# A two-layer decoder trunk: the norm's root applied ahead of the FFN's up products, the embedding's input product moved in front of them, and the convolution fed from PSUM

## Chip, cores and metric

The kernel runs on one core of one Trainium2 chip, in one launch. The metric is the device time of that core in microseconds; lower is better. A run before took 1123.33 us (median of three, 1122.11 to 1124.11).

## The reference, cut to what matters

The trunk has two layers over 512 positions with 1024 features (22 x 128 = 2816 in the FFN), all in float32. Layer 0 mixes by a gated MLP with spatial gating, layer 1 by sliding-window attention. Each layer then runs the same two blocks, and these are what the change touches:

```python
def rmsnorm(x, g):
    y = x * lax.rsqrt(jnp.mean(x * x, axis=-1, keepdims=True) + EPS)
    return y * g

def conv_ffn(xn, w_up, conv_w, conv_b, w_down):          # xn = rmsnorm(h, norm_ffn)
    h = xn @ w_up                                        # 1024 -> 2 * 2816
    hp = jnp.pad(h, ((0, 0), (CONV_WIDTH - 1, 0), (0, 0)))
    c = conv_b + sum(hp[:, t:t + S] * conv_w[t] for t in range(CONV_WIDTH))
    g, u = jnp.split(c, 2, axis=-1)
    return (jax.nn.silu(g) * u) @ w_down

def per_layer_embed(h, p_i, g_norm, w_in, w_gate, b_gate):
    gate = jax.nn.sigmoid(rmsnorm(h, g_norm) @ w_gate + b_gate)
    return (p_i @ w_in) * gate                           # added to h
```

The product `p_i @ w_in` depends on no other step of the layer, so it can be computed anywhere ahead of the gate.

## The kernel before, in words

**Layout and products.** Activations lie transposed, 128 features on the partitions by 512 positions: `h[0..7]` is the residual stream. Each float32 operand is split into a high part rounded to the matmul's type and a low remainder, and a product is three matmuls (high x high, low activation x high weight, high activation x low weight), all in `mm3`. The weight splits come out of `pump`: ACT casts the high part (`wh`, L197), DVE subtracts for the low part (`wl`, L198), 1024 columns at a time. Four buffers hold such pairs (WBUFS), three the raw weights. `plan` lists the weight pieces in the order of their use, and `load` and `pump` walk down that list, some units ahead of the products, on the SP queue. The order of instructions on each engine is made by a scheduler from the order in which the code issues them; `behind` adds an order by hand.

**The norm.** `Norm.take(k)` runs as each `h[k]` is finished: it splits `h[k]` times the gain into the tiles `xs` (ACT L302, DVE L303), squares it on ACT and adds up the squares (POOL, the last one on DVE). `turn` transposes and reduces the sum (`nf0quarter`), and `begin` sums over the partitions by a small matmul (`nf0ms`) and takes the root on POOL (`nf0rt`). The root belongs to a position, thus to a column of every tile, and must reach all partitions. `spread` does that with a matmul by ones into PSUM (`np0sp`); with `line=True` the root goes to HBM and comes back to all partitions by two DMAs of POOL (`nf0line`, `nf0rstd`). The FFNs used the second way: up products ran on input without the root, and each result was multiplied by the root afterwards.

**The FFN** (`ffn`) has 22 up products of 48 matmuls (24 for the gate half, 24 for the other half, each into its own PSUM bank). `gated` turns two banks into one activation: DVE multiplies by the root (`hs`, L551), ACT starts the convolution with the last tap and the bias (`c`, L557), DVE adds the two other taps (L558, L559), ACT applies silu, DVE multiplies the halves (`a`, L563). The down products come in three parts: after up 0 to 7 and up 8 to 15 in a woven form that saves multiplications (`woven_add`, products `dx` and `dy` of 256 columns), after up 16 to 21 as plain products (`dense_add`, `d`). One up product is always issued ahead of a woven part, to cover the last gate.

**The embedding.** `ple_in` (layer 0, products `pin`) and `ple_in_rows` (layer 1, `pint`) compute `p @ w_in` in 48 matmuls between up 21 and the `d` products, and ACT copies the results to `m0` to `m3` in SBUF, where they stay until the gate stage (`ple`, or the final stage of layer 1) multiplies them. The tiles `m0` to `m3` also hold operands of the woven products, and `m4`, `m5` the split input `p`.

Of the kernel before, what the change touches and what calls it, by code (L numbers as in the profile page):

```python
# [13 lines left out]
P = 128  # L14
# [36 lines left out]
def tile_yoco(ctx: ExitStack, tc: tile.TileContext, t, out: bass.AP, out_b: bass.AP):  # L51
# [29 lines left out]
    def plan_cols(w, n_chunks, kk, cols=256, k0=0):  # L81
        for c in range(n_chunks):
            plan(w[c, :, k0 * cols : (k0 + kk) * cols], kk * cols, cols)
# [11 lines left out]
            pieces.append((w[c, :, k0 * 256 : k1 * 256], 2 * n, [(0, n)] * 3 + [(0, n // 2)], None))  # L95

    def plan_ffn(l):
        for i, (j0, j1) in enumerate(PARTS):
            if i == 0:
                plan_cols(t["w_up"][l], j1, KD)  # L100
            else:
                plan_cols(t["w_up"][l, j0 + 1 : j1], j1 - j0 - 1, KD)
            if i + 1 < len(PARTS):
                plan_cols(t["w_up"][l, j1 : j1 + 1], 1, KD)
            else:
                plan(t["pT"][l], 2 * S, S, own=[(mp, "m4", "m5")])
# [211 lines left out]
    class Norm:  # L318


        def __init__(self, name, gains):
            self.name = name
# [64 lines left out]
        def spread(self, c0, n):  # L387

            d = tp.tile([P, n, 64], F32R, tag="acc", name=f"{self.name}d")
            nc.vector.tensor_mul(d, pick.rearrange("p (o t) -> p o t", o=1).to_broadcast([P, n, 64]),  # L390
                                 self.hl[:, c0 : c0 + n].bitcast(F32).rearrange("p (c o) -> p c o", o=1)
                                 .to_broadcast([P, n, 64]))
# [138 lines left out]
    def ffn(l, norm, nxt):  # L531

        xs = norm.xs[0][0]
        rstds = []
# [12 lines left out]
        def gated(j, pss, fronts=()):  # L547
            cs = []
            for s, ps in enumerate(pss):
                hs = tp.tile([P, S], F32, tag="hs", name=f"hs{j}_{s}")  # L550
                ins = nc.vector.tensor_mul(hs, ps, rstds[1])  # L551
                if fronts:
                    behind(ins, splits[fronts[s]][1])
# [3 lines left out]
                nc.scalar.activation(c, hs, AF.Identity, bias=v("conv_b", l * 2 * NJ + col), scale=cw[2])  # L557
                nc.vector.scalar_tensor_tensor(c[:, 1:], hs[:, : S - 1], cw[1], c[:, 1:], op0=ALU.mult, op1=ALU.add)  # L558
# [4 lines left out]
            nc.vector.tensor_mul(a, a, cs[1])  # L563
# [27 lines left out]
        return pe  # L591

    def ple_in(l):
        pw = chunk(S, 2)
        px = [(a[:, o : o + S], b[:, o : o + S]) for a, b, o in pw]
        pe = []
        for c in range(2):
            parts = chunk(256, 4)
            for q in range(2):
                pq = mp.tile([P, 2, S], F32, tag=f"m{2 * c + q}", name=f"pe{c}_{q}")  # L600
                for j in range(2):
                    ps = psum(f"pin{c}_{q}_{j}")
                    mm3(ps, parts[2 * q : 2 * q + 2], px, j * P)
                    nc.scalar.copy(pq[:, j, :], ps)
                    pe.append(pq[:, j, :])
        return pe

    def ple_in_rows():

        pw = chunk(S, 2)  # L610
        px = [(a[:, o : o + S], b[:, o : o + S]) for a, b, o in pw]
# [1 line left out]
        for c in range(2):  # L613
# [3 lines left out]
            for i in range(NC):  # L617
# [7 lines left out]
        return tok  # L625

    def ple(l, norm, nxt, pe):
        xs = norm.xs[0][0]
# [118 lines left out]
    for c in range(4):  # L747
# [4 lines left out]
        for j in range(2):  # L752
# [332 lines left out]
            with tc.high_priority():  # L1085
                weights(i)
    state["tags"] = [0, 1, 2]
    nf = Norm("nf1", [(xp, "x", gain("norm_ffn", 1))])
# [269 lines left out]
```

## Time and profile before

| what | us |
|---|---|
| median of three runs | 1123.33 |
| lowest, highest | 1122.11, 1124.11 |
| the profiled execution, its own time | 1120.52 |
| its span, first to last instruction | 1118.8 |

The profile is of one execution, and all times of rows are counted from its span's start. Some stages of it, in us from the start: the up products of layer 0 from 143.8, those of layer 1 from 700.3; pin at 465.45, pint at 1022.22. The granted clock of TensorE is 0.998 over the span. A row of a group gives engine, line, operation, output and inputs, then the number of instructions, their busy time, the mean in ns, and the idle time of the engine just before them with what ended it. A row of a timeline gives start, duration, engine, line, operation, tiles and shapes. A row of the chain of waits gives start, duration and what ran. A row of the stretches gives the stretch, its length, the busy time of PE, its weight loads, DVE, ACT and POOL with their counts, the clock, the DMA engines' share and GB/s. PE rows overlap: a matmul's duration goes to the end of its output, and the next begins before that.

### The profile page before, as it was taken

To read this page: it belongs to the slowest core of one execution; us is meant where nothing else is said; L and a number is where in the kernel's file an instruction comes from. 1 tells how busy PE (TensorE), PEld (TensorE's weight loads), DVE (VectorE), ACT (ScalarE), POOL (GpSimd) and SP (SyncE) were. 2 spreads that over 40 slices of the span, in tenths; PEclk is the share of its full clock that TensorE was granted. 3 is DMA by queue.
4 is the path that set the end of the run, shared out by engine and by line. 5 is a ranking of instruction groups with operands and counts; after the bars stand their busy time and mean duration, and the time that the engine had idled before them with its cause. 6 is when DMAs were issued, how large, how long until landed. Compare 5 with 4: busy or idle time off the path is not lost.

```text
span 1118.8 us, 14875 instructions
## 1 busy us (share of the span) xinstructions
PE 1108.8 (99%) x5691; PEld 947.1 (85%) x5691; DVE 868.3 (78%) x1374; ACT 568.9 (51%) x936; POOL 103.9 (9%) x167
## 2 busy tenths in 40 slices
PE   9999999999999999999999999999999999999997
PEld 7888888889888998888888887888898889988876
DVE  5566449999788877657988997499997898785696
ACT  5733325545444544554656776255454445445543
POOL 1100210000000000022204451100000000000210
PEclk9999999999999999999999999999999999999999
DMA  8632313223331252333134224321244212522433
GB/s 296 135 114 76 113 48 113 76 76 123 142 113 39 76 189 69 101 113 113 63 88 132 76 57 151 111 93 71 76 151 136 90 38 76 189 85 88 148 103 86
DMA packets 35624, 118.40 MB, mean 106 GB/s; under 512 B 11800, under 2 KB 17440, under 8 KB 25056
## 3 DMA queue, kind: packets, MB, share of 16 engines
q1 hardware_dynamic: 34800, 116.19, 31.8%
q0 software_dynamic: 336, 0.79, 0.4%
q8 instruction: 45, 0.74, 0.3%
q10 hardware_dynamic: 416, 0.46, 0.1%
q14 instruction: 27, 0.22, 0.1%
HBM read 109.02 MB, written 2.11 MB: 99 GB/s over the span
## 4 chain that ended last, share of the span: by engine, by line
PE 68%; DVE 20%; ACT 4%; DMA 4%; issue 3%; POOL 0%; POOLq 0%; SPq 0%; ACTq 0%; DVEq 0%
PE up L229 26%; PE d L229 7%; PE dx L229 5%; DVE wl L198 5%; PE dy L229 4%; PE gate L229 4%; PE u L229 4%; PE q L229 3%; DVE c L558 3%; DVE c L559 2%; PE o L229 2%; DVE hs L551 2%; ACT wh L197 1%; PE v L241 1%; PE v L239 1%
## 5 line engine op out<-in xcount | busy, mean ns | idle before, releaser
L198 DVE TENSOR_TENSOR wl<-wraw,wh 128x1024 fp32r<-128x1024 f32 (+2 forms) x198 | 232.8, 1177 | 83.4 <-ACT wh L197 82.1
L197 ACT CAST wh<-wraw 128x1024 fp32r<-128x1024 f32 (+2 forms) x197 | 194.1, 990 | 147.9 <-PE up L229 56.1
L229 PE MATMUL up<-nf00h,wh 128*128 128x512 f32 x352 | 137.1, 390 | 0.0
L229 PE MATMUL up<-nf10h,wh 128*128 128x512 f32 x352 | 137.0, 389 | 0.0
L229 PE MATMUL up<-nf10l,wh 128*128 128x512 f32 x352 | 137.0, 389 | 0.0
L229 PE MATMUL up<-nf00l,wh 128*128 128x512 f32 x352 | 137.0, 389 | 0.0
L229 PE MATMUL up<-nf00h,wl 128*128 128x512 f32 x352 | 136.9, 389 | 0.0
L229 PE MATMUL up<-nf10h,wl 128*128 128x512 f32 x352 | 136.9, 389 | 0.0
L557 ACT ACTIVATE c<-hs,vec 128x512 f32<-128x512 f32 x88 | 71.6, 815 | 64.4 <-DVE hs L551 62.6
L558 DVE SCALAR_TENSOR_TENSOR c<-hs,vec,c 128x511 f32<-128x511 f32 x88 | 65.5, 747 | 20.4 <-ACT c L557 20.4
L229 PEld LDWEIGHTS up<-nf10h,wh 128*128 128x128 f32 x352 | 66.1, 188 | 13.7
L229 PEld LDWEIGHTS up<-nf00h,wl 128*128 128x128 f32 x352 | 66.1, 188 | 13.7
L229 PEld LDWEIGHTS up<-nf10l,wh 128*128 128x128 f32 x352 | 66.1, 188 | 13.7
L229 PEld LDWEIGHTS up<-nf00l,wh 128*128 128x128 f32 x352 | 66.1, 188 | 13.6
L229 PEld LDWEIGHTS up<-nf00h,wh 128*128 128x128 f32 x352 | 66.1, 188 | 13.6
L229 PEld LDWEIGHTS up<-nf10h,wl 128*128 128x128 f32 x352 | 66.1, 188 | 13.5
L559 DVE SCALAR_TENSOR_TENSOR c<-hs,vec,c 128x510 f32<-128x510 f32 x88 | 65.6, 748 | 2.2
L197 ACT CAST wh<-wsum 128x1024 fp32r<-128x1024 f32 x32 | 33.7, 1052 | 35.3 <-PE dy L229 11.3
L551 DVE TENSOR_TENSOR hs<-up,nf1rstd 128x512 f32<-128x512 f32 x44 | 30.1, 686 | 21.1 <-DMA nf1rstd<-nf1line 10.5
L551 DVE TENSOR_TENSOR hs<-up,nf0rstd 128x512 f32<-128x512 f32 x44 | 30.1, 686 | 20.9 <-DMA nf0rstd<-nf0line 10.4
L198 DVE TENSOR_TENSOR wl<-wsum,wh 128x1024 fp32r<-128x1024 f32 x32 | 39.1, 1221 | 9.3 <-ACT wh L197 9.2
L562 ACT ACTIVATE a<-c 128x512 f32<-128x512 f32 x44 | 27.7, 630 | 15.9 <-DVE c L559 15.8
(519 smaller groups left out, 2661.4 us busy)
## 6 DMA issues: line engine op xcount, KB each, us to landing
wraw<-in_w_up SPq DMA_DIRECT2D x44, 1024.0 KB, 4.8
wraw<-in_w_down SPq DMA_DIRECT2D x16, 1024.0 KB, 4.8
wraw<-in_w_gate SPq DMA_DIRECT2D x8, 1024.0 KB, 5.3
wraw<-in_w_down SPq DMA_DIRECT2D x8, 768.0 KB, 4.1
wraw<-in_w_u SPq DMA_DIRECT2D x4, 1024.0 KB, 10.8
wraw<-in_w_out SPq DMA_DIRECT2D x4, 1024.0 KB, 4.7
wraw<-in_w_q SPq DMA_DIRECT2D x4, 1024.0 KB, 4.8
wraw<-in_w_o SPq DMA_DIRECT2D x4, 1024.0 KB, 4.9
```

The lines of the kernel that those rows point to most:

```text
L197: cast = nc.scalar.copy(hi, src)
L198: state["split"] = splits[u] = cast, nc.vector.tensor_sub(low, src, hi.bitcast(F32))
L229: nc.tensor.matmul(ps, w, x, start=first and j == 0, stop=last and j == len(todo) - 1, skip_group_check=onto)
L239: nc.tensor.matmul(ps, xh[:, s], wh[:, a:b], start=st, stop=False)
L241: nc.tensor.matmul(ps, xh[:, s], wl[:, a:b], start=False, stop=en)
L551: ins = nc.vector.tensor_mul(hs, ps, rstds[1])
L557: nc.scalar.activation(c, hs, AF.Identity, bias=v("conv_b", l * 2 * NJ + col), scale=cw[2])
L558: nc.vector.scalar_tensor_tensor(c[:, 1:], hs[:, : S - 1], cw[1], c[:, 1:], op0=ALU.mult, op1=ALU.add)
L559: nc.vector.scalar_tensor_tensor(c[:, 2:], hs[:, : S - 2], cw[0], c[:, 2:], op0=ALU.mult, op1=ALU.add)
L562: nc.scalar.activation(a, cs[0], AF.Silu)
```

## The change

1. The FFN's norms are made with `late=True` and no longer split `h` as it is finished. A new `Norm.scale` spreads the root by a matmul (`nf0sp`), and for each of the eight tiles DVE computes `x = h * gain * root` with the root read from PSUM, ACT copies the high part, DVE subtracts the low part. The two DMAs through `nf0line` are gone.
2. `pin` and `pint` are issued in front of up 0. `begin` stands after 18 of their 48 matmuls, `scale` after 36. The plan of weights moves accordingly.
3. Their results go from `m0` to `m3` to HBM (`keep`, DMAs on ACT's queue) and come back (`back`, DMAs on SP's queue, issued after up 18).
4. Up 0 runs through its eight inputs once and feeds both PSUM banks at each, where it ran all eight for one bank and then for the other. The order within an input is high activation with both weights, then the low activation.
5. `gated` has no `hs`: ACT and DVE read the up products from PSUM.
6. After up 21 the `d` products follow directly.

```diff
     def plan_ffn(l):
+        plan(t["pT"][l], 2 * S, S, own=[(mp, "m4", "m5")])
+        plan_cols(t["w_pin"][l], 2, 4)
...
-            else:
-                plan(t["pT"][l], 2 * S, S, own=[(mp, "m4", "m5")])
-                plan_cols(t["w_pin"][l], 2, 4)
...
         def take(self, k):
-            self.split(k, 0)
+            if not self.late:
+                self.split(k, 0)
...
+        def scale(self):
+            ps = self.spread(0, S // 64)
+            xs, g = self.xs[0]
+            u = state["next"]
+            for k in range(KD):
+                x = tp.tile([P, S], F32, tag="hs", name=f"{self.name}x{k}")
+                ins = nc.vector.scalar_tensor_tensor(x, h[k], g(k), ps, op0=ALU.mult, op1=ALU.mult)
+                if k % 4 == 0:
+                    behind(ins, splits[u + k // 4][1])
+                nc.scalar.copy(xs[k][0], x)
+                self.low = nc.vector.tensor_sub(xs[k][1], x, xs[k][0].bitcast(F32))
+            behind(splits[u + 2][1], self.low)
...
         def up(j, later=False):
             parts = chunk(256, KD)
-            pss = []
-            for s in range(2):
-                ps = psum(f"up{j}_{s}")
-                mm3(ps, parts, xs, s * P)
-                pss.append(ps)
-                if j == 0:
-                    rstds.append(norm.rstd() if s else norm.begin(rows=0, halves=False, line=True))
+            pss = [psum(f"up{j}_{s}") for s in range(2)]
+            if j:
+                for s in range(2):
+                    mm3(pss[s], parts, xs, s * P)
+            else:
+                for k, ((wh, wl, off), (xh, xl)) in enumerate(zip(parts, xs)):
+                    for x, both in ((xh, (wh, wl)), (xl, (wh,))):
+                        for s, ps in enumerate(pss):
+                            for w in both:
+                                nc.tensor.matmul(ps, w[:, off + s * P : off + (s + 1) * P], x,
+                                                 start=k == 0 and x is xh and w is wh, stop=k == KD - 1 and x is xl)
...
         def gated(j, pss, fronts=()):
...
-                hs = tp.tile([P, S], F32, tag="hs", name=f"hs{j}_{s}")
-                ins = nc.vector.tensor_mul(hs, ps, rstds[1])
...
-                nc.scalar.activation(c, hs, AF.Identity, bias=v("conv_b", l * 2 * NJ + col), scale=cw[2])
-                nc.vector.scalar_tensor_tensor(c[:, 1:], hs[:, : S - 1], cw[1], c[:, 1:], op0=ALU.mult, op1=ALU.add)
-                nc.vector.scalar_tensor_tensor(c[:, 2:], hs[:, : S - 2], cw[0], c[:, 2:], op0=ALU.mult, op1=ALU.add)
+                nc.scalar.activation(c, ps, AF.Identity, bias=v("conv_b", l * 2 * NJ + col), scale=cw[2])
+                for tap in (1, 2):
+                    ins = nc.vector.scalar_tensor_tensor(c[:, tap:], ps[:, : S - tap], cw[2 - tap], c[:, tap:],
+                                                         op0=ALU.mult, op1=ALU.add)
...
-        pe = None
+        kept = (ple_in_rows if l else ple_in)(l, norm)
         ahead = up(0)
+        behind(splits[state["next"] + 1][1], norm.low)
...
-            act += [whole(j - j0 - 1, j, up(j)) for j in range(j0 + 1, j1)]
-            pe = ple_in_rows() if l else ple_in(l)
+            for j in range(j0 + 1, j1):
+                act.append(whole(j - j0 - 1, j, up(j)))
+                if j == j0 + 2:
+                    back = [mp.tile([P, D], F32, tag=f"m{q}", name=f"back{q}") for q in range(NC)]
+                    for x, y in zip(back, kept):
+                        nc.sync.dma_start(x, y)
             dense_add(act, j1 - j0, nxt)
...
+    def keep(x, name):
+        y = dram.tile([P, D], F32, name=name)
+        nc.scalar.dma_start(y, x)
+        return y
...
     def ple_in(l, norm):
...
+                    if (c, q, j) == (0, 1, 0):
+                        norm.begin(rows=0)
+                    if (c, q, j) == (1, 0, 1):
+                        norm.scale()
+                pe.append(keep(pq, f"kept{c}_{q}"))
...
-    nf = Norm("nf0", [(xp, "x", gain("norm_ffn", 0))])
+    nf = Norm("nf0", [(xp, "x", gain("norm_ffn", 0))], late=True)
...
-            nf.split(m, 0)
             nf.square(m, nc.vector)
```

In the built program the order on the engines follows: after up 21, ACT casts two units of down weights ahead of the second `c`, and DVE makes their low parts ahead of its taps. In layer 0, ACT has the cast for up 2 ahead of the high parts of inputs 5, 6 and 7; in layer 1 it stands behind all eight. The loads of `back` stand on SP ahead of those for up 20 and 21.

More of the change, by code (lines that the diff above doesn't have):

```diff
@@ L318, in tile_yoco, with __init__ @@
     class Norm:
-        def __init__(self, name, gains):
-            self.name = name
+        def __init__(self, name, gains, late=False):
+            self.name, self.late = name, late
             self.xs = [(xtiles(pool, f"{name}{i}", tags), g) for i, (pool, tags, g) in enumerate(gains)]
@@ L556, in gated @@
                 c = tp.tile([P, S], F32, tag=f"c{s}", name=f"c{j}_{s}")
-                nc.scalar.activation(c, hs, AF.Identity, bias=v("conv_b", l * 2 * NJ + col), scale=cw[2])
-                nc.vector.scalar_tensor_tensor(c[:, 1:], hs[:, : S - 1], cw[1], c[:, 1:], op0=ALU.mult, op1=ALU.add)
-                nc.vector.scalar_tensor_tensor(c[:, 2:], hs[:, : S - 2], cw[0], c[:, 2:], op0=ALU.mult, op1=ALU.add)
+                nc.scalar.activation(c, ps, AF.Identity, bias=v("conv_b", l * 2 * NJ + col), scale=cw[2])
+                for tap in (1, 2):
+                    ins = nc.vector.scalar_tensor_tensor(c[:, tap:], ps[:, : S - tap], cw[2 - tap], c[:, tap:],
+                                                         op0=ALU.mult, op1=ALU.add)
+                    if fronts and tap == 1:
+                        behind(ins, splits[fronts[s]][1])
                 cs.append(c)
@@ L587, in ffn, with ple_in @@
             act = [whole(SLOTS - 1, j0, ahead)]
-            act += [whole(j - j0 - 1, j, up(j)) for j in range(j0 + 1, j1)]
-            pe = ple_in_rows() if l else ple_in(l)
-            dense_add(act, j1 - j0, nxt)
-        return pe
-    def ple_in(l):
+            for j in range(j0 + 1, j1):
[4 more added lines that the diff above has]
+                        nc.sync.dma_start(x, y)
+            dense_add(act, j1 - j0, nxt)
+        return back if l else [x[:, o : o + S] for x in back for o in (0, S)]
+    def keep(x, name):
+        y = dram.tile([P, D], F32, name=name)
+        nc.scalar.dma_start(y, x)
+        return y
+    def ple_in(l, norm):
         pw = chunk(S, 2)
@@ L599, in ple_in @@
             for q in range(2):
[L600 removed]
+                pq = mp.tile([P, D], F32, tag=f"m{2 * c + q}", name=f"pe{c}_{q}")
                 for j in range(2):
@@ L603, in ple_in, with ple_in_rows @@
                     mm3(ps, parts[2 * q : 2 * q + 2], px, j * P)
-                    nc.scalar.copy(pq[:, j, :], ps)
-                    pe.append(pq[:, j, :])
+                    nc.scalar.copy(pq[:, j * S : (j + 1) * S], ps)
+                    if (c, q, j) == (0, 1, 0):
[3 more added lines that the diff above has]
+                pe.append(keep(pq, f"kept{c}_{q}"))
         return pe
-    def ple_in_rows():
+    def ple_in_rows(l, norm):
         pw = chunk(S, 2)
@@ L624, in ple_in_rows @@
                 nc.scalar.copy(tok[i][:, c * S : (c + 1) * S], ps)
-        return tok
+                if (c, i) == (0, 2):
+                    norm.begin(rows=0)
+                if (c, i) == (1, 1):
+                    norm.scale()
+        return [keep(x, f"kept{i}") for i, x in enumerate(tok)]
     def ple(l, norm, nxt, pe):
@@ L1087, in tile_yoco @@
     state["tags"] = [0, 1, 2]
-    nf = Norm("nf1", [(xp, "x", gain("norm_ffn", 1))])
+    nf = Norm("nf1", [(xp, "x", gain("norm_ffn", 1))], late=True)
     for c in range(4):
```

3 lines of the change are left out of this document (removed).

## The prediction

> **What bounds the kernel now.** I read the page's head first, then the waits of TensorE (PE), then the chain that ended last, then the timelines of the places that the diff touches.
>
> ```profile
> span 1118.8 us, 14875 instructions
> PE 1108.8 (99%) x5691; PEld 947.1 (85%) x5691; DVE 868.3 (78%) x1374; ACT 568.9 (51%) x936; POOL 103.9 (9%) x167
> PE np1ms L361 <- DVE np1quarter L352: 0.5, 1, 0.5
> PE dy L229 <- DVE h L513: 0.4, 1, 0.4
> 283.25 87.07 PE up L229 x384
> 465.61 11.12 PE pin L229 x48
> ```
>
> PE is busy for 99% of the span, and the two longest waits that the profile names inside the work are 0.5 and 0.4 us. So the end is set by the number of matmuls and by the few places where PE stands still; no other engine's load counts by itself. The chain gives the rate: eight up products are 384 matmuls in 87.07 us, 0.227 us each (a single row shows 0.39 us because neighbours overlap). An up product of 48 takes 10.88 us, the embedding's input product (pin) 11.12 us. In the FFNs I compare the start of each matmul with the one before. Ahead of a dy or dx product six gaps are longer than the rate explains. The largest and the last are:
>
> ```profile
> 804.06 0.28 PE L229 MATMUL dx<-act,wl 128*128 128x256 f32 x1
> 804.79 0.39 PE L229 MATMUL dy<-act_0h,wh 128*128 128x256 f32 x1 [0.45 <-DVE h L513]
> 944.75 0.28 PE L229 MATMUL dy<-act_0l,wh 128*128 128x256 f32 x1
> 945.11 0.39 PE L229 MATMUL dx<-act_2h,wh 128*128 128x256 f32 x1
> ```
>
> A 256-column matmul follows the one before by 0.12 us, so these are 0.61 and 0.24 us lost; the other four lose 0.22 or 0.23 each. All six make 1.8 us, and that is all that a lighter VectorE (DVE) can give back to PE in both FFNs.
>
> **What goes, and why it is worth little.** Removed are the 88 products hs (all on DVE) and, per FFN, two DMAs of POOL that carried the root to all partitions; added per FFN are eight products x and one spreading matmul.
>
> ```profile
> L551 DVE TENSOR_TENSOR hs<-up,nf0rstd 128x512 f32<-128x512 f32 x44 | 30.1, 686 | 20.9 <-DMA nf0rstd<-nf0line 10.4 <-PE up L229 10.3
> L557 ACT ACTIVATE c<-hs,vec 128x512 f32<-128x512 f32 x88 | 71.6, 815 | 64.4 <-DVE hs L551 62.6
> L829 DVE SCALAR_TENSOR_TENSOR qf<-q,qscale,n1rstd 128x512 f32<-128x512 f32 x8 | 6.0, 748 | 1.2 <-PE q L229 1.1
> L558 DVE SCALAR_TENSOR_TENSOR c<-hs,vec,c 128x511 f32<-128x511 f32 x88 | 65.5, 747 | 20.4 <-ACT c L557 20.4
> L604 ACT COPY pe<-pin 128x512 f32<-128x512 f32 x8 | 4.7, 582 | 2.7 <-PE pin L229 2.7
> ```
>
> That is 60.2 us off DVE (44 x 0.686, twice), some 12 us back (16 x 0.75), and none of it was on PE. Even DVE's 10.4 us wait for the root cost PE nothing: no gap lies there. Of the 1.8 us above I credit half, **-0.9** (bounds 0 and -1.8), since such a gap can also be a weight that is only just prepared. The taps now read PSUM. A scalar_tensor_tensor of this size takes 748 ns where its source is the PSUM product (qf) and 747 where it is SBUF (c), so I price that at zero. [...]
>
> The two spreading matmuls are pure PE work: 2 x 0.227 = **+0.45**. The 96 matmuls of pin only move. The four new DMAs to HBM per FFN stand on ACT's queue; the only DMA issue on ACT in the trace took 0.46 us. They and the four loads back (on SP, ahead of the loads for up 20 and 21) move 2 MB each way in stages where the DMA engines are busy 0.24 and 0.32 of the time (the last column but one of the stretches):
>
> ```profile
> 0.80 0.46 ACTq L167 DMA_DIRECT2D wraw<-in_w_v  x1
> 143.00:249.00 106.00, 105.93 (x496) 88.59 (x495) 84.96 (x126) 49.28 (x66) 2.99 (x3) 1.00 0.24 82
> 411.00:466.00 55.00, 55.00 (x245) 45.53 (x244) 39.67 (x49) 25.23 (x32) 0.00 (x0) 1.00 0.32 108
> 411.18 54.43 PE up L229 x240
> wraw<-in_w_up SPq DMA_DIRECT2D x44, 1024.0 KB, 4.8
> ```
>
> SP holds the loads of up 20 and 21 until the woven products that read the same buffers end, at 411.18; up 20 starts three up products later, at 443.8, and a load lands 4.8 us after its issue. The results themselves are wanted only in the gate stage, behind all the d products. So the transfers are hidden: zero, and some 5 us for a late one if that cover were gone.
>
> **The end of each FFN: the cover that goes.** Until now pin ran on PE between the last up product (up 21) and the last group of down products (d). Here is what ran beside it in layer 0:
>
> ```profile
> 465.22 0.39 PE L229 MATMUL up<-nf00h,wl 128*128 128x512 f32 x1
> 465.45 0.62 PE L229 MATMUL pin<-own_m,wh 128*128 128x512 f32 x2
> 465.42 0.84 ACT L197 CAST wh<-wraw 128x768 fp32r<-128x768 f32 x1 [1.26 <-PE up L229]
> 466.37 0.82 ACT L557 ACTIVATE c<-hs,vec 128x512 f32<-128x512 f32 x1
> 466.29 0.96 DVE L198 TENSOR_TENSOR wl<-wraw,wh 128x768 fp32r<-128x768 f32 x1
> 467.22 0.75 DVE L558 SCALAR_TENSOR_TENSOR c<-hs,vec,c 128x511 f32<-128x511 f32 x1
> 468.79 0.69 DVE L563 TENSOR_TENSOR a<-a,c 128x512 f32<-128x512 f32 x1
> 469.52 0.62 ACT L306 CAST act21h<-a 128x512 fp32r<-128x512 f32 x1 [0.51 <-DVE a L563]
> 470.17 0.69 DVE L307 TENSOR_TENSOR act21l<-a,act21h 128x512 fp32r<-128x512 f32 x1 [0.69 <-ACT act21h L306]
> 1022.22 0.40 PE L621 MATMUL pint<-wh,own_m 128*128 128x512 f32 x1
> 1026.95 0.69 DVE L307 TENSOR_TENSOR act21l<-a,act21h 128x512 fp32r<-128x512 f32 x1 [0.69 <-ACT act21h L306]
> ```
>
> In the changed kernel d follows up 21 directly, so its first matmul starts at 465.45. Its first output sums six activations of three matmuls each, act21 last: 15 x 0.227 = 3.40 us later, at 468.85, it wants act21h, and one matmul later act21l. The order of the built kernel keeps a cast of down weights ahead of the convolution's start c on ACT, and that weight's low part ahead of the taps on DVE. The cast waits for up 21 to release its buffer (465.42). So leaving hs out does not start c or the taps earlier by more than 0.1 us, and act21h still ends at 470.14, act21l at 470.86. PE waits 470.14 - 468.85 = 1.3 us, runs one matmul, and waits 0.5 more: 1.8 us. Layer 1 has the same queues and the same distances (its act21l starts 1026.95, 4.73 us after pin's start at 1022.22; in layer 0 it is 4.72). Two FFNs: **+3.6**. Bounds: if ACT served c ahead of the cast, at the 0.58 us of a PSUM copy, the chain would be 0.2 + 0.58 + two taps at 0.79 + 0.69 + 0.62 and four handoffs of 0.05, 3.9 us to act21h: 0.7 us with the low part. If one more weight unit came between (0.84 and 0.96), 2.7 us. I take 1.8, the row's own order.
>
> **The start of each FFN: the new path.** The up products used to begin on unscaled input. Now the sum of squares, the root, its spreading, the scaling and the split all lie ahead of them, under pin. Before (nf0, layer 0) and for a norm that spreads by a matmul already (np0):
>
> ```profile
> 143.79 0.48 PE L229 MATMUL up<-nf00h,wh 128*128 128x512 f32 x1
> 145.92 0.73 DVE L303 SCALAR_TENSOR_TENSOR nf00l<-h,vec,nf00h 128x512 fp32r<-128x512 f32 x1
> 148.04 0.69 DVE L352 TENSOR_REDUCE nf0quarter<-nf0turn 128x16 f32<-128x512 f32 x1
> 514.65 0.29 PE L361 MATMUL np0ms<-np0quarter,alike 128*128 128x16 f32 x2
> 515.74 1.68 POOL L414 TENSOR_TENSOR np0rt<-np0m,minus_half 128x8 f32<-128x8 f32 x1 [7.01 <-DVE np0m L412]
> 517.85 0.70 DVE L390 TENSOR_TENSOR np0d<-pick,np0hl 128x512 fp32r<-128x512 f32 x1
> 700.25 1.06 ACT L197 CAST wh<-wraw 128x1024 fp32r<-128x1024 f32 x1 [0.52 <-PE o L229]
> 700.28 0.39 PE L229 MATMUL up<-nf10h,wh 128*128 128x512 f32 x1
> 701.63 1.22 DVE L198 TENSOR_TENSOR wl<-wraw,wh 128x1024 fp32r<-128x1024 f32 x1
> ```
>
> *Mean square (ms).* PE reaches it after 18 matmuls of pin, 143.79 + 4.08 = 147.87. The reduce ended at 148.73; without the split ahead of it (nf00l, 0.68 net) it ends at 148.05: 0.2 us of stall. In layer 1 PE comes at 700.28 + 4.08 = 704.36. DVE now puts a weight's low part first: cast to 701.31, wl to 702.55, then the last sum, the transpose and the reduce, 2.1 us from the end of nf00l to that of the reduce, 704.7: 0.35.
>
> *Root to spread.* In np0 the operand was ready 518.55 - 514.65 = 3.9 us after ms. Here 18 matmuls and ms itself, 4.2 us, lie between: no stall.
>
> *Scaling.* The first up product starts 12 matmuls (2.72 us) after the spread; call that U. It takes the eight inputs in turn, six matmuls (1.36 us) each. DVE makes x (0.75) and the low part (0.69), 1.44 per input, but starts 2.3 us ahead; ACT copies the high part (0.62). In layer 1 that suffices for all eight (16 instructions of 0.72: the last low part is ready at U + 9.2, wanted four matmuls into input 7, at U + 10.4). In layer 0 the built order has on ACT, ahead of the high parts 5 to 7, a cast into the buffer that up 0 itself reads until its fourth input: U + 5.44, cast 1.05, copy 0.62, a handoff 0.05: U + 7.16, wanted at U + 6.80: 0.36. Input 7 follows through two low parts, x and a copy at U + 10.0, wanted at U + 9.88: 0.1. The next product's low weights, queued behind all of that, come 0.1 late. So layer 0 loses 0.2 + 0.6 = 0.8, layer 1 0.35: **+1.15** (bounds 0, all under pin, and 4.2, the second rival).
>
> **Sum.** -0.9 + 0.45 + 3.6 + 1.15 = +4.3 us. The profiled execution took 1120.52 us with a span of 1118.8, so 1124.8 on its own account; it was 2.8 us under the median of the runs, 1123.33, to which I add the sum: **1127.6 us**, 0.38% slower. Its own range, with each term half of the way to its bounds, is 1125.5 to 1130.4.
>
> **Rivals.**
> *Not slower: the last gate fits.* If c and the taps of up 21 pass the weights on ACT and DVE, the end costs 0.7 per FFN; with all of the 1.8 us regained and nothing lost at the start it is 1.4 + 0.45 - 1.8 = 0: 1123.4. It decides where act21h comes within about 3.9 us of the last up matmul. For it speaks ACT's 62.6 us of waits for hs, which go; against it the cast that waits for the same last matmul. Chance 0.13.
> *The scaling does not keep pace.* If each x waits for its low part's buffer and for ACT's copies and DMA issues (0.46 each), an input costs DVE 1.7 to 1.8 us instead of 1.44, 8 x 0.3 = 2.4 us less a lead of about 0.9 (1.2 in layer 1 by the above, less in layer 0), 1.5 more in each FFN: +7.3, 1130.6. It decides above about 1.55 us per input. For it: the 1.44 already exceeds PE's 1.36; against: the order alternates pairs, so that DVE seldom waits. Chance 0.17.
> *Faster by relief.* If PE loses time to a busy DVE in ways that starts of matmuls do not show, 48 us less could give some back; at -1.8 and with the ends hidden, 1120 to 1121. The 87.07 us for 384 matmuls, while DVE was as busy as anywhere, speak against it. Chance 0.04.
> My forecast has the remaining 0.66.
>
> **Numbers.** The range runs from 1124.4 (most of the first rival left out) to 1131.5 (the second rival and the upper bounds). Within 0.2% (2.2 us, about what a measurement of this kernel can tell from no change) lie the first rival and the low edge of the forecast: 0.14; faster by more 0.04; slower by more 0.82.
>
> **What would show it.** In the changed profile: PE waits for act21h and act21l, some 1.3 and 0.5 us, ahead of the sixteenth and seventeenth d matmul, in both layers; small waits at ms and, in layer 0, at inputs 5 and 7 of up 0; DVE busy near 820 us; no wait for HBM. A d stage that follows up 21 without a gap, or waits over 1 us within up 0, would make me wrong.

## The result, and the profile after

The changed kernel took 1119.11 us (median of 11, 1118.89 to 1121.14), the kernel before on the same chip 1121.97 (median of 11, 1120.20 to 1124.11): a ratio of 0.9976, 95% interval 0.9968 to 0.9985. It is faster by 0.24%, 2.9 us; on a second chip the ratio was 0.9968 (0.9956 to 0.9980). The forecast was 0.38% slower. The profiled execution after took 1119.28 us. One execution of all that follow, the profiled one of `no_root_no_hs`, ran slow (1220.34 us at a granted clock of 0.85), so that its ratio leaves it out and no gap is read from it.

The page after: span, busy times, the share of each engine in the chain that ended last, and the rows of the convolution and of the results' way back.

```profile
span 1117.5 us, 14886 instructions
PE 1108.6 (99%) x5693; PEld 947.8 (85%) x5693; DVE 826.9 (74%) x1308; ACT 564.7 (51%) x936; POOL 101.8 (9%) x163
...
PE 96%; DVE 2%; issue 1%; ACT 1%; DMA 0%; POOLq 0%; POOL 0%
...
L572 DVE SCALAR_TENSOR_TENSOR c<-up,vec,c 128x510 f32<-128x510 f32 (+1 forms) x176 | 130.5, 746 | 32.5 <-ACT c L570 30.4
...
L570 ACT ACTIVATE c<-up,vec 128x512 f32<-128x512 f32 x88 | 68.1, 776 | 49.8 <-PE up L228 44.6
...
back<-kept SPq DMA_DIRECT2D x8, 512.0 KB, 4.4
```

PE has two matmuls more than before and the same busy time (1108.6 us for 1108.8); the span fell by 1.3 us, so what went is time in which PE stood. The taps take 746 ns from PSUM, as the prediction had it (747 from SBUF). These are all waits of PE that the profile of after names, the first of them ahead of the first product:

```profile
PE idle L277 <- DVE minus_half L280: 1.1, 1, 1.1
PE sc L1015 <- PE sc L1016: 0.2, 1, 0.2
PE np1ms L361 <- DVE np1quarter L352: 0.2, 1, 0.2
```

The wait for `h` ahead of dy is gone, and no wait for act21h, for `back` or within up 0 took its place. Compared start by start, all six gaps of the woven products (1.76 us in the first profile of before) are gone; new is 0.20 ahead of layer 1's ms.

### The profile page after: what moved, and what is told of

It reads as the page before. It is cut to its first block, busy times and chain, and to the rows that moved or that the text cites. A ratio compares the mean times of both kernels' runs of the same rounds, so it can differ in the third digit from the quotient of the medians.

```text
span 1117.5 us, 14886 instructions
## 1 busy us (share of the span) xinstructions
PE 1108.6 (99%) x5693; PEld 947.8 (85%) x5693; DVE 826.9 (74%) x1308; ACT 564.7 (51%) x936; POOL 101.8 (9%) x163
## 4 chain that ended last, share of the span: by engine, by line
PE 96%; DVE 2%; issue 1%; ACT 1%; DMA 0%; POOLq 0%; POOL 0%
PE up L228 41%; PE d L228 9%; PE dx L228 8%; PE dy L228 6%; PE q L228 4%; PE gate L228 4%; PE u L228 4%; PE o L228 3%; PE up L560 2%; PE v L238 1%; PE v L240 1%; PE v L239 1%; PE pin L228 1%; PE k L228 1%; PE pv L1083 1%; PE gt L238 1%
## 5 line engine op out<-in xcount | busy, mean ns | idle before, releaser
L572 DVE SCALAR_TENSOR_TENSOR c<-up,vec,c 128x510 f32<-128x510 f32 (+1 forms) x176 | 130.5, 746 | 32.5 <-ACT c L570 30.4
L228 PE MATMUL up<-nf00h,wh 128*128 128x512 f32 x336 | 130.7, 389 | 0.0
L228 PE MATMUL up<-nf10h,wh 128*128 128x512 f32 x336 | 130.7, 389 | 0.0
L228 PE MATMUL up<-nf00l,wh 128*128 128x512 f32 x336 | 130.7, 389 | 0.0
L228 PE MATMUL up<-nf10l,wh 128*128 128x512 f32 x336 | 130.7, 389 | 0.0
L228 PE MATMUL up<-nf10h,wl 128*128 128x512 f32 x336 | 130.5, 389 | 0.0
L228 PE MATMUL up<-nf00h,wl 128*128 128x512 f32 x336 | 130.4, 389 | 0.0
L570 ACT ACTIVATE c<-up,vec 128x512 f32<-128x512 f32 x88 | 68.1, 776 | 49.8 <-PE up L228 44.6
L228 PEld LDWEIGHTS up<-nf00h,wl 128*128 128x128 f32 x336 | 63.1, 188 | 13.2
L228 PEld LDWEIGHTS up<-nf10h,wh 128*128 128x128 f32 x336 | 63.1, 188 | 13.1
L228 PEld LDWEIGHTS up<-nf10h,wl 128*128 128x128 f32 x336 | 63.1, 188 | 13.1
L228 PEld LDWEIGHTS up<-nf00h,wh 128*128 128x128 f32 x336 | 63.1, 188 | 13.0
L228 PEld LDWEIGHTS up<-nf00l,wh 128*128 128x128 f32 x336 | 63.1, 188 | 12.9
L228 PEld LDWEIGHTS up<-nf10l,wh 128*128 128x128 f32 x336 | 63.1, 188 | 12.9
L196 ACT CAST wh<-wsum 128x1024 fp32r<-128x1024 f32 x32 | 33.7, 1053 | 39.3 <-PE dx L228 10.5
L445 DVE TENSOR_TENSOR h<-h,d 128x512 f32<-128x512 f32 x24 | 16.4, 682 | 21.5 <-PE d L228 21.5
L1027 ACT ACTIVATE prs<-prs,neg 128x129 f32<-128x129 f32 x64 | 25.3, 397 | 13.4 <-DVE neg L1022 12.7
L579 DVE TENSOR_TENSOR a<-a,c 128x512 f32<-128x512 f32 x44 | 30.4, 690 | 1.7 <-ACT a L578 0.2
```

Source lines behind the costliest of these rows:

```text
L196: cast = nc.scalar.copy(hi, src)
L228: nc.tensor.matmul(ps, w, x, start=first and j == 0, stop=last and j == len(todo) - 1, skip_group_check=onto)
L445: nc.vector.tensor_add(h[m], h[m], ps)
L570: nc.scalar.activation(c, ps, AF.Identity, bias=v("conv_b", l * 2 * NJ + col), scale=cw[2])
L572: ins = nc.vector.scalar_tensor_tensor(c[:, tap:], ps[:, : S - tap], cw[2 - tap], c[:, tap:], op0=ALU.mult, op1=ALU.add)
L1027: ins = nc.scalar.activation(pr[:, e, :], pr[:, e, :], AF.Exp, bias=neg[:, e : e + 1], scale=-1.0, accum_out=sm[:, e : e + 1])
```

## The experiments

Five questions, each with its runs. Ratios are to the kernel before on the same chip, with 95% intervals.

**1. Where did the 3.6 us at the end of the FFNs go?** First the timelines of after, layer 0, around the sixteenth d matmul (start, duration, engine):

```profile
479.57 0.39 PE L228 MATMUL d<-act20h,wl 128*128 128x512 f32 x1
479.79 0.39 PE L228 MATMUL d<-act16h,wh 128*128 128x512 f32 x1
...
480.40 0.62 ACT L305 CAST act21h<-a 128x512 fp32r<-128x512 f32 x1 [2.52 <-DVE a L579]
480.93 0.39 PE L228 MATMUL d<-act17h,wl 128*128 128x512 f32 x1
481.06 0.69 DVE L306 TENSOR_TENSOR act21l<-a,act21h 128x512 fp32r<-128x512 f32 x1 [0.69 <-ACT act21h L305]
481.16 0.41 PE L228 MATMUL d<-act21h,wh 128*128 128x512 f32 x1
481.41 0.40 PE L228 MATMUL d<-act18h,wh 128*128 128x512 f32 x1
...
481.88 0.42 PE L228 MATMUL d<-act21l,wh 128*128 128x512 f32 x1
```

act21h is ready at 481.02 and act21l at 481.75. d starts at 476.39, so that is 4.63 and 5.36 us later; the prediction had 4.69 and 5.41. But after fifteen matmuls of the first output the built order has six of the second (act16, act17), then the first output's act21h, two more of the second, then act21l. PE does not stand at all. To price what this order hides, the first output's eighteen matmuls were forced to run in a row (`d_in_order`):

```diff
-                mm3(ps, parts, xs, j * P)
+                begun, ended = mm3(ps, parts, xs, j * P)    # first and last matmul of an output
+                if kk < KD and m:
+                    behind(begun, state["ended"])
+                state["ended"] = ended
...
```

> The changed kernel, with each output of the last down products (d, after up 16 to 21) held back by an order on TensorE until the output before it is finished, so that no matmul of the next output can fill a wait. If the end of an FFN was mis-sized only because the scheduler fills the wait for act21 with matmuls of the next output, the two waits of 1.3 and 0.5 us come back in both layers: 3.6 us more than the changed kernel, ratio to before about 1.001 (the changed kernel: 0.9976). If act21 is ready in time anyway, nothing changes: 0.9976.

Measured: 1123.34 us, ratio 1.0006 (0.9997 to 1.0014), 3.4 us above the changed kernel's 0.9976. The waits of PE in it:

```profile
PE d L228 <- ACT act21h L308: 2.2, 2, 1.1
...
PE d L228 <- DVE act21l L309: 0.4, 2, 0.2
```

Start by start the gaps are 1.28 and 0.49 us in layer 0, 1.27 and 0.50 in layer 1: 3.54 in all, against the 3.6 of the prediction. The chain was sized rightly; that it reached PE was wrong.

**2. What does the root's trip through HBM cost?** The root spread by a matmul in the kernel before, all else as it was (`root_by_matmul`):

```diff
-                    rstds.append(norm.rstd() if s else norm.begin(rows=0, halves=False, line=True))
+                    rstds.append(norm.rstd() if s else norm.begin(rows=0))
```

> The kernel before, with the FFN's root spread by a matmul (as the embedding's norm does) in place of the two DMAs of GpSimd; hs, the place of pin and everything else as before. Theory A (the root's trip through HBM varies from one execution to the next, and a late one makes VectorE late for the weights): most of the gain appears, ratio 0.998 and a narrower spread of the runs than before's. Theory B (the hs products load VectorE, and the gaps ahead of dx and dy come from that): nothing or +0.45 us for the two matmuls, ratio 1.000.

1121.38 us, ratio 0.9988 (0.9979 to 0.9996). The gaps ahead of the first dy (0.23 and 0.61 in the first profile of before) are gone, the four ahead of dx are all there at 0.23. Then the other way, the trip made longer by one DMA (`root_trip_doubled`):

```diff
+                if self.name.startswith("nf"):
+                    twin = dram.tile([S], F32, name=f"{self.name}twin")
+                    nc.gpsimd.dma_start(twin, self.line)
+                    self.line = twin
                 nc.gpsimd.dma_start(r, self.line.partition_broadcast(P))
```

> The kernel before, with one DMA more in each FFN's trip of the root (line to a second line in HBM, then to all partitions); nothing else. Theory A (DVE has no time to spare between the root's arrival and the first woven part, so a later root moves the first dy): the added leg, by the rows of the two legs there are 4 to 8 us, shows as a gap ahead of the first dy of each FFN, less what DVE catches up on the way; 2 to 7 us per FFN, 4 to 14 in all, ratio 1.004 to 1.013 to before. Rival (the trip is hidden; what the change gained came from the products hs alone): ratio 1.000, the gaps ahead of the first dy as before, 0.2 and 0.6 us.

1132.92 us, ratio 1.0086 (1.0072 to 1.0099): 9 to 10 us. Waits of DVE for the root, and of PE, in it:

```profile
DVE hs L555 <- DMA nf1rstd<-nf1twin: 14.8, 1, 14.8
DVE hs L555 <- DMA nf0rstd<-nf0twin: 13.1, 1, 13.1
...
PE up L229 <- ACT wh L197: 3.4, 2, 2.5
...
PE dy L229 <- DVE h L517: 1.3, 2, 0.8
PE up L229 <- DVE wl L198: 1.2, 2, 0.6
```

In layer 0 DVE waits 2.7 us longer than in the first profile of before, and PE stands not only ahead of the first dy: ACT's casts of up weights are queued behind the convolution's start `c`, which waits for hs, so up products wait for their weights too. By starts of matmuls these waits cost 2.2 us more than the first profile of before lost in layer 0, and 3.8 in layer 1, where DVE waits 4.3 us longer. They are not the whole: after them the clock granted to TensorE is half for 3.4 us in each layer (the last column but two of the stretches), and the up products start 0.43 us apart instead of 0.227, which makes some 1.6 us more in each.

```profile
180.00:183.40 3.40, 3.40 (x10) 2.63 (x9) 3.33 (x6) 1.35 (x2) 0.00 (x0) 0.50 0.17 19
743.20:746.60 3.40, 3.37 (x8) 2.69 (x9) 3.37 (x5) 1.36 (x2) 0.00 (x0) 0.50 0.01 2
```

So the trip was at the edge of costing PE time. It also varies. The kernel before was therefore profiled three more times, and the changed kernel once.

> The kernel before, unchanged, for a second profiled execution: where the usual execution, some 2 us above the one profiled first, spends them. Theory A (the root's trip through HBM varies, and a later root shifts PE): a usual execution (1122 to 1124 us) shows a trip longer than 12 us and PE gaps among up 2 to up 4 or ahead of the first dy, 1 to 2.5 us more than the 0.8 of the first profile. Rival (the spread comes from elsewhere, such as attention's transposes waiting for DVE or the start): the gaps of the FFNs are as in the first profile, 1.8 us in all, and the excess lies in the attention stage or ahead of the first product.

The third and the fourth profile had the same expectations.

> As the second look at the kernel before: a third execution of it. Theory A: time and trip go together, about 1 us of PE gaps for each us by which the root comes later. Rival: they do not.

> The changed kernel, unchanged, for a second profiled execution. Theory A: no gap over 0.25 us in the FFNs, whatever its time. Rival: if its time is above 1120 us, the excess lies in the same places outside the FFNs as in the kernel before.

They took 1123.07, 1123.48 and 1124.85 us, close to the median. Two views of the third execution (1123.48): waits, then the timeline of PE at the first dy of layer 0.

```profile
DVE hs L551 <- DMA nf0rstd<-nf0line: 11.6, 1, 11.6
DVE hs L551 <- DMA nf1rstd<-nf1line: 11.3, 1, 11.3
...
PE dy L229 <- DVE h L513: 2.6, 2, 1.3
```

```profile
247.88 0.28 PE L229 MATMUL dx<-act,wl 128*128 128x256 f32 x1
249.48 0.38 PE L229 MATMUL dy<-act_0h,wh 128*128 128x256 f32 x1 [1.33 <-DVE h L513]
```

That gap is 1.48 us where the first profile had 0.23. The four executions side by side, layer 0 / layer 1:

| execution (us) | DVE waits for the root | gap ahead of the first dy |
|---|---|---|
| 1120.52 | 10.4 / 10.5 | 0.23 / 0.61 |
| 1123.07 | 11.0 / 11.1 | 0.89 / 1.25 |
| 1123.48 | 11.6 / 11.3 | 1.48 / 1.42 |
| 1124.85 | 11.4 / 11.3 | 1.30 / 1.45 |

In this table PE loses about one us per us by which the root comes later: between its arrival and the first woven part, some 80 us on, DVE never catches up. The mean of the four is 2.16 us for both layers, not the 0.84 of the profile that the prediction used. The second profile of the changed kernel, 1118.73 us, has no gap over 0.25 us in the FFNs.

**3. What makes the other four gaps, 0.92 us, ahead of dx?** They stayed in `root_by_matmul`. With hs put back into the changed kernel, as a product with a tile of ones (`after_with_hs`), they did not return:

```diff
-            for s, ps in enumerate(pss):
+            for s, bank in enumerate(pss):
+                ps = tp.tile([P, S], F32, tag="hs", name=f"hs{j}_{s}")
+                nc.vector.tensor_mul(ps, bank, unit)
...
+        unit = tp.tile([P, S], F32, tag="rstd", name="unit")
+        nc.gpsimd.memset(unit, 1.0)
```

> The changed kernel with one product put back: DVE multiplies each PSUM bank of an up product by a tile of ones into hs, and c and the taps read hs from SBUF, as before the change; the root is still applied ahead of the up products. Theory B (the products hs make the gaps ahead of dx<-act_2h and its like): four gaps of 0.23 us come back and the ratio to before rises from 0.9976 to 0.9984 to 0.9990. Theory A alone (all of the gain is the root's trip): ratio 0.997 to 0.998, no such gaps. If DVE's whole load counted, the ratio would be 1.000.

1120.38 us, ratio 0.9974 (0.9965 to 0.9983), no such gap. So neither hs as such (theory B) nor the trip makes them. In the kernel before, ACT's copy of a dx bank (260.00 to 260.36) ends just ahead of the late matmul at 260.41, with only two matmuls of edge (the operand of the next output's first product) and two of dy put between. `woven_order` put all twelve of edge there; `woven_order_root_by_matmul` did the same without the trip, beside a second set of runs of the changed kernel.

```diff
-                product(4, chain, w, 0, first=False)
+                begun, _ = product(4, chain, w, 0, first=False)
+                if front:
+                    behind(begun, front)        # front: the last matmul of the next output's product 1
...
```

> The kernel before with one order added on PE: the product that ends a woven output (the second one of act_2 on a dx bank) stands behind all twelve matmuls of the next output's first product (edge), where the built order had two of them and two of dy. Theory C (the four gaps of 0.23 us are PE waiting for ACT's copy of that bank, tail, because the built order puts too little between; the changed kernel's order happens to put more): the four gaps go, the first dy gaps stay, 0.9 us less, ratio 0.9990 to 0.9995. Rival B (the gaps are DVE's load by the products hs): the gaps stay or move, ratio 1.000.

> The same order added to the kernel before with the root spread by a matmul; the products hs, the place of pin and the unscaled input stay as before the change. Theories A and C together: neither the gaps ahead of the first dy nor the four of 0.23 us; 1.3 and 0.9 us less, ratio 0.9978 to 0.9983, within 0.6 us of the changed kernel on the same chip. If taking hs off DVE or scaling the input counts by itself, it stays 1 us or more above the changed kernel.

> The changed kernel, for a comparison on the same chip with the two others: ratio 0.997 to 0.998.

Ratios 1.0033 (1.0022 to 1.0045), 1.0023 (1.0014 to 1.0032) and, for the changed kernel, 0.9968 (0.9956 to 0.9980). Theory C fell: the order made it worse, and the wait of PE in `woven_order` says why.

```profile
PE dx L229 <- DVE wl L198: 4.2, 4, 1.1
```

Matmuls of edge need low weights that DVE has not made yet. That the scheduler had put the closing product ahead for this reason is inferred; 0.23 us was the smaller loss. So the question became what makes these low weights late. The change has a line about just that, which neither its list nor the parts of the diff shown above contain: the hand-written order of the last gate of a woven part held hs behind two earlier low weights, and now holds the first tap.

```diff
+                    if fronts and tap == 1:
+                        behind(ins, splits[fronts[s]][1])
```

That one line was moved in the kernel before (`tap_held`), in the kernel without the trip (`tap_held_root_by_matmul`), and back in the changed kernel with hs (`after_hs_held`):

```diff
-                ins = nc.vector.tensor_mul(hs, ps, rstds[1])
-                if fronts:
-                    behind(ins, splits[fronts[s]][1])
+                nc.vector.tensor_mul(hs, ps, rstds[1])
...
+                ins = nc.vector.scalar_tensor_tensor(c[:, 1:], hs[:, : S - 1], cw[1], c[:, 1:], op0=ALU.mult, op1=ALU.add)
+                if fronts:
+                    behind(ins, splits[fronts[s]][1])
```

> The kernel before with one line moved: the hand-written order of the last gate of a woven part (gated with fronts) holds the first tap behind the low weights, as in the changed kernel, and no longer the product hs. Theory D (this line sets the order on DVE and PE in the woven parts, and with the old place the next low weights come late, which woven_order showed as 1.2 us of PE waiting for wl): the four gaps of 0.23 us go, PE runs eight or more matmuls of the next output ahead of the closing product; 0.9 us less or somewhat more, ratio 0.9985 to 0.9993; the first dy gaps remain with the root's trip. Rival B (the load of the products hs on DVE makes them): the gaps stay, ratio 1.000.

> The same line moved in the kernel before with the root spread by a matmul. Theories A and D together: no gap over 0.2 us in the FFNs, ratio 0.9970 to 0.9980, within 0.7 us of the changed kernel, though pin stands behind up 21, the products hs are all there and the input is unscaled. If scaling the input, moving pin or a lighter DVE earn something by themselves, it stays 1 us or more above the changed kernel (0.9968 and 0.9976 on two chips).

> The changed kernel with the product hs back (by a tile of ones) and the order held at hs, as before the change; beside after_with_hs, where hs is back and the tap is held. Theory D: the four gaps come back, 0.9 us above after_with_hs, ratio 0.998 to 0.9986. Rival B: as after_with_hs, 0.9974, without the gaps.

| | hs held | tap held |
|---|---|---|
| root by DMA | 1 (the kernel before) | 1.0046 (1.0032 to 1.0059) |
| root by matmul, input unscaled | 0.9988 (0.9979 to 0.9996) | 0.9975 (0.9966 to 0.9984) |
| changed kernel with hs | 0.9988 (0.9980 to 0.9997) | 0.9974 (0.9965 to 0.9983) |
| changed kernel, no hs | (no hs) | 0.9976 (0.9968 to 0.9985) and 0.9968 (0.9956 to 0.9980) |

Wherever the tap is held the four gaps are gone, and wherever hs is held they are there (0.22 or 0.23 each in `after_hs_held`). DVE's timelines show how. First `root_by_matmul`, then `tap_held_root_by_matmul`; the last row of each is the late low weight.

```profile
251.33 0.68 DVE L551 TENSOR_TENSOR hs<-up,nf0rstd 128x512 f32<-128x512 f32 x1
...
254.43 0.68 DVE L551 TENSOR_TENSOR hs<-up,nf0rstd 128x512 f32<-128x512 f32 x1
...
260.55 1.23 DVE L198 TENSOR_TENSOR wl<-wraw,wh 128x1024 fp32r<-128x1024 f32 x1
```

```profile
238.46 0.68 DVE L551 TENSOR_TENSOR hs<-up,nf0rstd 128x512 f32<-128x512 f32 x1
...
242.83 0.69 DVE L551 TENSOR_TENSOR hs<-up,nf0rstd 128x512 f32<-128x512 f32 x1 [0.64 <-PE up L229]
...
258.65 1.21 DVE L198 TENSOR_TENSOR wl<-wraw,wh 128x1024 fp32r<-128x1024 f32 x1
```

Held, the two hs of this gate run in the full stretch between low weights; free, they run ahead of it and of the first dy, and the low weight starts 1.9 us earlier (some 1.2 of it the two hs, the rest a sum of weights that now stands behind it). PE's first matmul of edge that reads a low weight shows what follows, in the same two runs: it ran behind the closing product and the gap, and now runs ahead of that product without one.

```profile
262.00 0.28 PE L229 MATMUL dx<-edge,wl 128*128 128x256 f32 x1
```

```profile
260.37 0.28 PE L229 MATMUL dx<-edge,wl 128*128 128x256 f32 x1
```

That needs a DVE that is on time there. With the trip it is not: in `tap_held` the second of these hs starts at 245.54, 2.7 us later than above, with the work on `h` that the first dy waits for still behind it, and the same line costs 5 us.

```profile
PE dy L229 <- DVE h L513: 3.8, 2, 2.0
...
PE dx L229 <- ACT head L509: 1.0, 2, 0.7
```

By starts of matmuls these waits make 5.4 us, 2.4 more than the six gaps of before on average. In layer 1 the granted clock is again 0.5 for 3.4 us behind them (812.9 to 816.3), some 1.6 us more. The rest of the 5 us is not traced.

**4. Do the other parts of the change earn or cost anything?** Taking root, trip and hs out of the kernel before altogether, so that the FFN lacks the norm's root (`no_root_no_hs`; here too the tap was held):

> The kernel before, with the multiplication by the root left out of both FFNs (no hs, no trip of the root, the convolution reads PSUM; the FFN's output lacks the norm's root); pin stays behind up 21. It has the relief of VectorE without the new path at the start. Theories A and B both give the whole gain: six gaps of 1.8 us go in the profile, ratio 0.997 to 0.998. If instead the place of pin or the order of up 0 brings the gain, ratio 1.000.

Ratio 0.9975 (0.9964 to 0.9985): as the changed kernel. Moving pin and its results' way through HBM alone, with the trip and hs kept (`pin_ahead_only`):

```diff
+        kept = ple_in_rows() if l else ple_in(l)
         ahead = up(0)
...
-            pe = ple_in_rows() if l else ple_in(l)
...
```

> The kernel before, with the embedding's input product moved ahead of up 0, its results taken through HBM, and d following up 21 directly; root, trip and hs as before. Theories A and B: no gain, ratio 1.000 (0.999 to 1.001), the gaps ahead of dx and dy as before. If the place of pin brings the gain: 0.9976.

Ratio 1.0005 (0.9996 to 1.0014); its first-dy gaps are 0.50 and 1.44, the four of dx remain. Up 0 bank after bank in the changed kernel (`up0_bank_by_bank`), and the results written and read twice (`kept_trip_doubled`):

```diff
-                for k, ((wh, wl, off), (xh, xl)) in enumerate(zip(parts, xs)):
-                    ...
+                for s in range(2):
+                    mm3(pss[s], parts, xs, s * P)
```

```diff
+                        nc.sync.dma_start(x, y)        # each back loaded twice
...
+        z = dram.tile([P, D], F32, name=name + "twin")
+        nc.scalar.dma_start(z, x)                      # each result written to a second place
```

> The changed kernel with up 0 in its old order: all eight inputs for one PSUM bank, then all eight for the other, so each input is wanted 0.68 us after the one before instead of 1.36. If the scaling only just keeps pace (as the prediction had it, 1.44 us of DVE per input with a lead of 2.3 us): PE waits within up 0, 8 x 1.44 less 8 x 0.68 less the lead, some 3 to 4 us per FFN, 6 to 8 in all, ratio 1.003 to 1.005 to before. If the order of up 0 plays no part: 0.9976 as the changed kernel.

> The changed kernel with the embedding's results written to HBM twice and loaded back twice (8 more DMAs per FFN: 4 on ACT's queue, 4 on SP's). If the trip is hidden: ratio 0.9976 to before, as the changed kernel. If the DMA issues on ACT (0.46 us each) or the loads ahead of the weights for up 20 and 21 cost something: above 0.9985.

Ratios 0.9967 (0.9954 to 0.9979) and 0.9964 (0.9951 to 0.9976): no cost in either. The 6 to 8 us expected of the first did not come: PE's rows show no gap within up 0. The built order mixes its matmuls otherwise than the code does (three of high activation and high weight stand in a row at 159.66), so here too the order of the code is not the one that runs. Why up 0 of the changed kernel never stalls is seen in its timelines of layer 0:

```profile
161.46 1.05 ACT L196 CAST wh<-wraw 128x1024 fp32r<-128x1024 f32 x1 [1.71 <-PE up L560]
162.41 1.14 ACT L407 CAST nf00h<-nf0x 128x512 fp32r<-128x512 f32 x2
...
162.17 0.61 PE L560 MATMUL up<-nf00l,wh 128*128 128x512 f32 x2
162.62 0.39 PE L228 MATMUL up<-nf00h,wh 128*128 128x512 f32 x1
...
163.30 0.39 PE L228 MATMUL up<-nf00l,wh 128*128 128x512 f32 x1
163.53 0.39 PE L560 MATMUL up<-nf00h,wh 128*128 128x512 f32 x1
```

The cast does stand ahead of the high part of the sixth input, which is ready at about 163.03 where six inputs in turn would want it at 162.62. But L228 is up 1: four of its matmuls on inputs that are ready are put in there, 0.91 us, and up 0 (L560) goes on at 163.53.

**5. The rest of the spread.** Three of the four executions of before, and none of the three of the unaltered changed kernel, also lose 1.3 to 1.9 us at the transposes of layer 1's attention, which the change does not touch. The waits in that stage, first in the slowest execution of before (1124.85), then in the second of the changed kernel (1118.73):

```profile
PE tr L1022 <- DVE prs L1007: 1.4, 2, 1.1
...
ACT wh L197 <- DMA wraw<-in_w_q: 3.3, 1, 3.3
```

```profile
ACT wh L196 <- DMA wraw<-in_w_q: 1.3, 1, 1.3
```

One load of w_q lands late. In the profiles where ACT waits 3.1 us or more for it PE loses 1.3 us or more at the transposes; with 1.9 or less it loses nothing there; two profiles between, with 2.4 and 2.8, lose 0.6 and 1.0. `after_with_hs`, `after_hs_held`, `up0_bank_by_bank` and `tap_held_root_by_matmul` had it late as well, so it is no matter of the trip or the order. Whether the change makes it rarer is open; no run changed that load.

## Why the prediction was wrong

*The end of each FFN (+3.6): the step that failed.* The times of act21h and act21l were right to 0.1 us. Wrong was the step "Its first output sums six activations of three matmuls each, act21 last: 15 x 0.227 = 3.40 us later, at 468.85, it wants act21h". That takes PE through the outputs one after the other as the code lists them. The order of ACT and DVE had been read in the built program, PE's had not. Measured: 0, since matmuls of the second output stand in front of act21h and act21l; forced into the code's order, PE waited 3.54 us. Without this step the sum would have been +0.7.

*The start (+1.15).* Of the 0.8 in layer 0 nothing came. For the 0.6 within up 0 it is the same step again: the sixth input was late about as forecast (0.41 us for 0.36), but up 1 fills. For the 0.2 at ms, PE came there at 148.31, not at 147.87, and found the operand ready. Layer 1's ms lost 0.20 of the 0.35. Together 0.2.

*The regained gaps (-0.9).* The mechanism that was doubted was the right one, and its size was too low for two reasons: halved without need, and taken from an execution 2.8 us under the median, with no question of where those 2.8 us lay. All six gaps went. In four executions they make 2.16 + 0.92 = 3.08 us on average. "Even DVE's 10.4 us wait for the root cost PE nothing: no gap lies there" was wrong: its price is paid 80 us later, at the first dy. For the other four, the doubt ("a weight that is only just prepared") pointed the right way but was used to halve the gain: the change moves the line of order that made this weight late, and the prediction gave that line no term.

*The spreading matmuls (+0.45)* stood: two more matmuls on PE. *The transfers (0)* stood, also doubled; the new issues on ACT took 0.33 or 0.34 us each. (The one of 0.46 us was not the only issue on ACT before: `out<-yt` at 1114.77 took 0.36.) *The taps from PSUM (0)* stood.

With these sizes the sum is -3.1 + 0.45 + 0.2 = -2.4 us, against 2.9 measured; the late load of w_q (1.15 us on average in the four profiles of before) and a shorter wait at np1ms (0.31 for 0.60 in the first profiles) can make up the difference, and which does is not settled. The rival "faster by relief" gave the right side, with a chance of 0.04, but not the cause: nothing was lost in ways that starts of matmuls do not show. Nor did the lighter DVE count by its 41 us (868.3 to 826.9), since hs put back costs less than these runs can tell (0.9974, beside 0.9967 and 0.9964 of the two other forms of the changed kernel on that chip). What counts is when the root comes, and where two products stand in one stretch. Two small edits to the kernel before, the root by matmul and one line of order, give 0.9975, which cannot be told from the whole change.

## What to carry to other kernels

Where a scheduler orders the engines, read the built order of the engine that sets the end before charging it a wait: a late operand cost nothing here where other ready matmuls stood in front of it (act21h and act21l: 0, against 3.54 us in the order of the code). Ask of a DMA on the path of a busy engine where that engine has its next pause; if it has none until a point where PE needs it, each us of delay can be paid there, here 80 us on (a root that came 1.2 us later, a gap of 1.48 us for 0.23). And compare the profiled execution with the median before sizing a gap: what the usual run loses can be missing from a lucky profile (0.84 us ahead of the first dy in it, 2.16 on average of the four).

## What the runs showed of the hardware

The write of the root to HBM, 2 KB from 64 partitions, took 8.6 us from issue to landing in the first profile of before and 9.9 in the third, more than the 256 KB that came back after it (3.7 and 3.6):

```profile
nf0rstd<-nf0line POOLq DMA_DIRECT2D x1, 256.0 KB, 3.6
nf0line<-nf0rt POOLq DMA_DIRECT2D x1, 2.0 KB, 9.9
```

ACT waited 1.9 us for one load of 1 MB of w_q in the first profile of before, where the load landed 6.2 us after its issue, and 3.3 us for the same load in the slowest execution, where PE waited 1.4 us at the transposes and in the first not at all.

Some waits of PE had a loss behind them beyond their own length. In `root_trip_doubled` (both layers) and in layer 1 of `tap_held`, pairs of waits of 0.8 to 2.7 us were followed by 3.4 us at a granted clock of 0.5; in layer 0 of `tap_held` a wait of 2.1 us, with one of 0.45 ahead of it, left the clock at 1.00. What decides between the two, these runs do not show.
